# The last pair of heads' column tiles, two at a time: first half of the tokens of both, then the second half of both

## The chip, the cores and the metric

One core of a Trainium2 chip. The time is device microseconds of one execution of the whole program on that core, lower is better. The engines are TensorE (PE: matmuls; PEld: its weight loads), VectorE (DVE), ScalarE (ACT), GpSimd (POOL) and SyncE (SP), which issues the DMAs.

## The reference

A hybrid block on x of 1024 tokens by 1024 channels, all in float32. A normalised input h goes through one wide projection w_in. Its columns feed a gated MLP branch (result ya), an RWKV-7 branch (result yb) and two gates:

```python
p = p + mu * (token_shift(p) - p)          # pb: columns r, k, v, z of the RWKV branch
o = wkv7_scan(r_h, w_h, k_h, v_h, kk, a_h) # 16 heads of 64, one state per head, along 1024 tokens
o = group_norm(o) * gn_g + gn_b + bonus
yb = o * silu(z)
...
merged = sigmoid(ga) * (ya @ w_a) + sigmoid(gb) * (yb @ w_b)
out = x + rms_norm(merged @ w_o, g_post)
```

The token shift reads the token before, so the second half of the tokens needs the last column of the first half.

## The kernel before

Tokens are the free dimension, channels the partitions. Two halves of 512 tokens; a *column tile* is 128 output channels. `gemm` (line 714) makes one column tile of one half: 8 blocks of 128 input channels, three matmuls each of 128x128 against 128x512 (the high parts, high against low, low against high), 24 matmuls into one PSUM bank "ps". The operand of the projections lies in 32 SBUF buffers of one pool ("hm": 8 blocks, high and low part, two halves). A weight column comes through `load_w` (line 701): one DMA to "raw" (one buffer), ACT writes the high part "whi", DVE or POOL the low part "wlo" (two buffers of each).

Stage 1 is the gated MLP. Stage 2 (pool "rw") is the RWKV branch: 8 pairs of heads, p = 0 to 7, each with four column tiles in the order k, r, v, z, and for each pair two *units* (p, h), one per token half, made by `half_unit` (line 426). A column tile is evacuated by `shifted` (line 1027): ACT scales the PSUM bank, DVE adds the bank shifted by one token, and the first half leaves its last column in "edge" for the second half.

A unit (p, h) prepares K, B and the decays; PE makes products of them (W·BK), DVE masks them to Pm and BA; Pm goes through DRAM (bs_d) into X, from which POOL solves a triangular system in 62 instructions on Q and qt; the result goes through DRAM (ts_d) into N; DVE transposes N into Pm, PE makes N·Pm and Pm·N, X·Pm, BA·X, and then a chain of eight small steps (pc<-Z,W) carries the state along the tokens. The normed and gated result oc is stored to yb_d.

Behind the last pair the 32 hm buffers are loaded with ya (ya_d, 32 loads of 256 KB, the first half's 16 first), each when the last matmul that reads the buffer's old content is done. Sixteen gemms with w_a follow (`jobs`); their results are gated on DVE (tile "r") and stored to ma_d. The projections with w_b and w_o are Strassen products (`product`): blocks of yb come back from DRAM, DVE and POOL add and subtract them (the *train* of additions), ACT and DVE split the sums, PE multiplies. w_a's gemms need no yb.

The order of every engine is made when the program is built, by a list scheduler (`Sched.flush`, line 240). Each operation has a priority (chain 0, evacuation and inverse 1, splits and loads 2, dense matmuls 9, last); among the operations that by its model can start soonest on their engine it takes the one of best priority, then the one that comes first in the program. A buffer's next owner waits for its last reader. So dense gemms fill what the units leave free on PE, and the engines run the resulting lists in order. SP's list is one queue: a DMA whose operand is late holds up all DMAs behind it.

Every operation is issued through a helper, so the profile puts all of them on line 134; they are told apart by tile names.

Of the kernel before, what the change touches and what calls it, by code (L numbers as in the profile page):

```python
# [21 lines left out]
KT = D // P  # L22
# [39 lines left out]
class Sched:  # L62
# [45 lines left out]
    @contextlib.contextmanager  # L108
    def at(self, prio):
        old, self.prio = self.prio, prio  # L110
        yield
        self.prio = old
# [544 lines left out]
def body(S, I, out):  # L657
    with contextlib.ExitStack() as stack:
        trunk(S, stack.enter_context, I, out)


def trunk(S, enter, I, out):
# [29 lines left out]
    def col(base, i):  # L692
        return vec[:, base + i:base + i + 1]
# [7 lines left out]
    def load_w(src, page=None, raw_page=None, later=0, hi_eng=None):  # L701
        raw = raw_page(F32) if raw_page else wp.tile([P, 1024], F32, name="raw", bufs=1)
        with at(W_DMA + later):
            dma(raw, src)
        hi, lo = [page(F32R) if page else wp.tile([P, 1024], F32R, name=nm, bufs=2) for nm in ("whi", "wlo")]
        with at(W_SPLIT + later):
            if hi_eng is not None:
                hi_eng.tensor_copy(hi, raw)
            else:
                act(hi, raw, AF.Copy)  # L710
            A.tensor_tensor(lo, raw, hi, op=ALU.subtract)
        return hi, lo
# [13 lines left out]
    def gemm_ct(w, rh, rl, dest=()):  # L726
        for h in range(2):
            ps = gemm(w, rh, rl, h, dest[h:h + 1])
            with at(EVAC):
                yield slice(512 * h, 512 * h + 512), ps  # L730
# [10 lines left out]
    with S.pool("gm") as gp:  # L741
        def page(dtype=F32, shape=(P, T)):
            return gp.tile(list(shape), dtype, name="pg", bufs=17, fifo=False)

        def ring(dtype):
            return gp.tile([P, 1024], dtype, name="ring", bufs=4)
# [4 lines left out]
        for i, n in enumerate((128, 128, 256, 256, 256)):  # L751
# [3 lines left out]
            if n == 128:  # L755
                x = gp.tile([P, KT, n], F32, name="z") if i == 0 else ring(F32).rearrange("p (k n) -> p k n", k=KT)
# [32 lines left out]
        def row(nm, shape=(P, T), dtype=F32, bufs=1):  # L789
            return gp.tile(list(shape), dtype, name=nm, bufs=bufs)  # L790
# [45 lines left out]
        for g in range(KT):  # L836
            for b in range(KT):
                x = vt[g][:, b, :]
# [121 lines left out]
        for d in range(2):  # L960
            w = load_w(I["w_in"][GA + d])
# [33 lines left out]
        for k in range(4):  # L995
            v1, v2 = row("th"), page()
# [25 lines left out]
    with S.pool("rw") as rw:  # L1022
# [1 line left out]
        V.tensor_scalar(hv[:, 0:32], vec[:, V_W0:V_W0 + 32], 0.5, None, op0=ALU.mult)  # L1024
        V.tensor_scalar(hv[:, 32:40], vec[:, V_KA:V_KA + 8], -0.5, 1.0, op0=ALU.mult, op1=ALU.add)

        def shifted(ct, w, tiles):

            for sl, ps in gemm_ct(w, hh, hl, tiles):
                t_ = tiles[0 if sl.start == 0 else 1]  # L1030
                act(t_, ps, AF.Identity, scale=om[:, ct:ct + 1])
                V.scalar_tensor_tensor(t_[:, 1:512], ps[:, 0:511], col(V_MU, ct), t_[:, 1:512],
                                       op0=ALU.mult, op1=ALU.add)
                if sl.start == 0:
                    edge = rw.tile([P, 1], F32, name="edge", bufs=2)
                    V.tensor_scalar(edge, ps[:, 511:512], col(V_MU, ct), None, op0=ALU.mult)
                else:
                    V.tensor_tensor(t_[:, 0:1], t_[:, 0:1], edge, op=ALU.add)

        RW0 = 2 * KT  # L1040
        order = [4 * KT] + [ct for p in range(KT) for ct in (KT + p, p, 2 * KT + p, 3 * KT + p)]

        def dense():

            w = wn
            for i, ct in enumerate(order):
                nw = load_w(I["w_in"][RW0 + order[i + 1]] if i + 1 < len(order) else I["w_a"][0])
                yield ct, w
                w = nw
            yield None, w  # L1050

        tiles = dense()

        xw, xa = rw.tile([P, T], F32R, name="xw"), rw.tile([P, T], F32R, name="xa")
        wa = rw.tile([P, T], F32, name="X", bufs=2, fifo=False)
        shifted(*next(tiles), [wa[:, 0:512], wa[:, 512:1024]])
        act(wa[0:64, :], wa[0:64, :], AF.Tanh)
        act(xw[0:64, :], wa[0:64, :], AF.Copy)
# [17 lines left out]
        for p in range(KT):  # L1076
            def halves(nm, bufs):
                return [rw.tile([P, 512], F32, name=nm, bufs=bufs) for _ in range(2)]

            k2, r2, v2, z2 = halves("k0", 2), halves("r", 3), halves("v", 2), halves("zz", 3)  # L1080
            for x in (k2, r2, v2, z2):
                shifted(*next(tiles), x)
            up = rw.tile([P, 2 * P], F32, name="hk")
            uh, ul = rw.tile([P, 2 * P], F32R, name="uh"), rw.tile([P, 2 * P], F32R, name="ul")
            with at(W_DMA):
                dma(up, I["up"][:, p])
            with at(PREP):
                G.tensor_copy(uh, up)
                A.tensor_tensor(ul, up, uh, op=ALU.subtract)
            for h in range(2):  # L1090
                sl = slice(512 * h, 512 * h + 512)
                Znext = half_unit(S, I, rw, dram, bank, p, h, r2[h], k2[h], v2[h], z2[h], uh, ul, bdr, xw[:, sl], xa[:, sl],
                                  Znext, KI[h], vec, con, hv, eps, yb_d[p][:, sl])
# [11 lines left out]
        _, wn = next(tiles)  # L1105
# [37 lines left out]
        def parts(xs):  # L1143
            return [part(x) for x in xs]
# [7 lines left out]
        def loaded(src):  # L1152
            x = unit()
            with at(W_DMA):
                dma(x, src)
            return x
# [48 lines left out]
        def wo(n):  # L1205

            xs = []
            for k in R4:
                t, hi, lo = pair_tile()
                with at(W_DMA):  # L1210
                    dma(t.bitcast(F32), wo_d[n][k])
                xs.append((hi, lo))
            return xs
# [53 lines left out]
        e2, r2 = parts(f2), wo(1)  # L1267
# [45 lines left out]
        x = {b: [loaded(I["x"][P * b:P * b + P, hs[e]]) for e in range(2)] for b in (0, 1, 2, 3, 4, 5, 6, 7)}  # L1313
# [68 lines left out]
```

## Time and profile before

| | us |
|---|---|
| median of 3 runs | 1429.69 (1426.26 to 1430.96) |
| the profiled execution | 1426.28 |
| its span | 1424.1 |
| PE busy in the span | 1347.4 |
| DVE, ACT, POOL busy | 1118.8, 742.6, 525.8 |

The span runs from the first to the last instruction; 2.2 us of the execution lie around it. The profile gives every instruction's start and duration, what ended the idle time before it, and the clock that was granted to TensorE (1.00 is 2.4 GHz, 0.50 is 1.2 GHz). Busy time on PE includes slow matmuls, so both columns are read together: idle time, and clock.

### The profile page before, as it was taken

The numbers are of one execution on the slowest core, as the hardware profiler recorded it, in microseconds if no ns is written. First come the engines' busy times: TensorE is split into PE (matmuls) and PEld (weight loads), VectorE is DVE, ScalarE is ACT, GpSimd is POOL, SyncE is SP. The second block draws the span as 40 slices with busy tenths as digits, with TensorE's granted clock in tenths as the row PEclk, the third lists the DMA queues.
The fourth block names the chain that finished last, engine by engine and source line by source line (L and its number), as shares of the span: only waits on it lengthen the run. The fifth ranks groups of instructions, "written<-read, shape, count | busy, mean of one in ns | idle before, by whom it ended". The sixth has DMA issues, their size and how long they took to land.

```text
span 1424.1 us, 23358 instructions
## 1 busy us (share of the span) xinstructions
PE 1347.4 (95%) x8390; PEld 1075.0 (75%) x8390; DVE 1118.8 (79%) x2034; ACT 742.6 (52%) x1340; POOL 525.8 (37%) x1135
## 2 busy tenths in 40 slices
PE   5899999999999999999998989999899899979997
PEld 3787888888878777777776767777677677858785
DVE  7977888887865868888788877888788575599957
ACT  6626444444444656667655567666666353433223
POOL 0002000001121176756566663776745553043211
PEclk9899999999999999999999999999999899989999
DMA  7102434447775211222211212211135756254456
GB/s 250 45 1 96 155 134 148 141 140 228 263 249 205 64 56 38 67 71 67 64 46 45 57 53 64 61 54 48 53 99 165 230 177 226 88 202 170 140 215 242
DMA packets 109523, 175.12 MB, mean 123 GB/s; under 512 B 43488, under 2 KB 53856, under 8 KB 109408
## 3 DMA queue, kind: packets, MB, share of 16 engines
q1 hardware_dynamic: 109408, 173.64, 36.8%
q8 instruction: 66, 1.08, 0.3%
q14 instruction: 49, 0.40, 0.1%
HBM read 121.17 MB, written 52.43 MB: 122 GB/s over the span
## 4 chain that ended last, share of the span: by engine, by line
PE 67%; DVE 13%; ACT 9%; DMA 6%; issue 4%; SPq 1%; POOL 1%; DVEq 0%; ACTq 0%; POOLq 0%
PE ps L134 37%; PE pg L134 25%; PE pc L134 5%; DVE hm L134 2%; DVE Pm L134 2%; ACT L134 2%; DVE W L134 1%; DMA hm<-ya_d 1%; DVE pg L134 1%; ACT Z L134 1%; DVE BK L134 1%; DVE wlo L134 1%; SPq L134 1%; ACT BA L134 1%; ACT KI L134 1%
## 5 line engine op out<-in xcount | busy, mean ns | idle before, releaser
L134 PE MATMUL ps<-hm,whi 128*128 128x512 f32 x1616 | 538.7, 405 | 5.3 <-DMA hm<-ya_d 4.7
L134 PEld LDWEIGHTS ps<-hm,whi 128*128 128x128 f32 x1616 | 301.8, 191 | 69.9 <-DMA hm<-ya_d 9.8
L134 PE MATMUL ps<-hm,wlo 128*128 128x512 f32 x808 | 326.8, 405 | 1.1 <-DVE wlo L134 1.1
L134 POOL TENSOR_TENSOR qt<-X,Q 128x60 f32<-128x60 f32 (+24 forms) x496 | 204.5, 412 | 91.3 <-DMA X<-bs_d 39.0
L134 POOL TENSOR_TENSOR Q<-Q,qt 128x60 f32<-128x60 f32 (+24 forms) x496 | 196.1, 395 | 37.9
L134 PEld LDWEIGHTS ps<-hm,wlo 128*128 128x128 f32 x808 | 154.1, 191 | 33.6 <-DVE wlo L134 3.1
L134 PE MATMUL pg<-pg,ring 128*128 128x512 f32 x720 | 168.1, 389 | 0.0
L134 PEld LDWEIGHTS pg<-pg,ring 128*128 128x128 f32 x720 | 135.1, 188 | 28.1
L134 ACT ACT_TABLE_LOAD x75 | 96.2, 1283 | 2.9 <-DVE mv L134 0.9
L134 ACT ACTIVATE whi<-raw 128x1024 fp32r<-128x1024 f32 x64 | 67.4, 1053 | 56.4 <-PE ps L134 30.0
L134 ACT ACTIVATE Z<-pc,gc 64x64 f32<-64x64 f32 x120 | 36.8, 307 | 106.9 <-PE pc L134 104.7
L134 DVE TENSOR_TENSOR wlo<-raw,whi 128x1024 fp32r<-128x1024 f32 x60 | 74.3, 1238 | 10.1 <-ACT whi L134 9.9
L134 POOL TENSOR_TENSOR th<-th 128x512 f32<-128x512 f32 x3 | 4.2, 1406 | 185.2 <-DMA pg<-in_w_o_dram 175.6
L134 ACT ACTIVATE X<-pg 128x512 f32<-128x512 f32 x64 | 36.9, 594 | 43.5 <-PE pg L134 43.0
L134 PE MATMUL ps<-pg,hm 128*128 128x512 f32 x192 | 50.9, 422 | 9.2 <-ACT pg L134 4.4
L134 DVE TENSOR_SCALAR Z<-pc,gc 64x64 f32<-64x64 f32 x120 | 34.8, 290 | 27.1 <-ACT Z L134 19.5
L134 PEld LDWEIGHTS pc<-Z,W 128*128 128x128 f32 x240 | 40.1, 188 | 20.2 <-DVE Z L134 8.3
L134 PEld LDWEIGHTS ps<-pg,hm 128*128 128x128 f32 x192 | 38.3, 202 | 20.2 <-ACT pg L134 5.0
L134 PE MATMUL pc<-Z,W 128*128 128x128 f32 x240 | 50.8, 293 | 1.1 <-ACT Z L134 0.4
L134 POOL TENSOR_TENSOR wlo<-raw,whi 128x1024 fp32r<-128x1024 f32 x4 | 9.9, 2479 | 112.7 <-DVE pg L134 85.0
L134 PE MATMUL pg<-W,BK 64*128 64x128 f32 (+1 forms) x530 | 47.3, 290 | 2.6 <-ACT KI L134 1.6
L134 PEld LDWEIGHTS pg<-W,BK 64*128 64x128 f32 (+1 forms) x530 | 37.7, 187 | 13.9 <-issue 5.4
(793 smaller groups left out, 2738.2 us busy)
## 6 DMA issues: line engine op xcount, KB each, us to landing
raw<-in_w_in_dram SPq DMA_DIRECT2D x65, 512.0 KB, 3.4
X<-bs_d SPq DMA_DIRECT2D x64, 128.0 KB, 2.7
hm<-ya_d SPq DMA_DIRECT2D x32, 256.0 KB, 5.4
wo_d<-sv SPq DMA_DIRECT2D x12, 512.0 KB, 2.7
raw<-in_w_a_dram SPq DMA_DIRECT2D x12, 512.0 KB, 3.3
W<-wo_d SPq DMA_DIRECT2D x10, 512.0 KB, 4.8
sv<-sv_d SPq DMA_DIRECT2D x8, 512.0 KB, 3.3
ya_d<-th SPq DMA_DIRECT2D x8, 512.0 KB, 2.6
```

What stands on the lines that cost most here:

```text
L134: self.calls.append(lambda: getattr(e, op)(*a, **k))
```

## The change

`shifted` becomes a generator, `shifting`, that stops after each half; `shifted` runs it to its end, as before. For p = 0 to 6 nothing changes. For the last pair the tiles are taken two at a time, first k and r, then v and z, and their halves alternate: k0, r0, k1, r1, v0, z0, v1, z1, in place of k0, k1, r0, r1, v0, v1, z0, z1 (the digit is the token half).

```diff
--- before.py
+++ after.py
@@ -1024,7 +1024,7 @@
         V.tensor_scalar(hv[:, 0:32], vec[:, V_W0:V_W0 + 32], 0.5, None, op0=ALU.mult)
         V.tensor_scalar(hv[:, 32:40], vec[:, V_KA:V_KA + 8], -0.5, 1.0, op0=ALU.mult, op1=ALU.add)
 
-        def shifted(ct, w, tiles):
+        def shifting(ct, w, tiles):
 
             for sl, ps in gemm_ct(w, hh, hl, tiles):
                 t_ = tiles[0 if sl.start == 0 else 1]
@@ -1036,6 +1036,11 @@
                     V.tensor_scalar(edge, ps[:, 511:512], col(V_MU, ct), None, op0=ALU.mult)
                 else:
                     V.tensor_tensor(t_[:, 0:1], t_[:, 0:1], edge, op=ALU.add)
+                yield
+
+        def shifted(ct, w, tiles):
+            for _ in shifting(ct, w, tiles):
+                pass
 
         RW0 = 2 * KT
         order = [4 * KT] + [ct for p in range(KT) for ct in (KT + p, p, 2 * KT + p, 3 * KT + p)]
@@ -1078,8 +1083,15 @@
                 return [rw.tile([P, 512], F32, name=nm, bufs=bufs) for _ in range(2)]
 
             k2, r2, v2, z2 = halves("k0", 2), halves("r", 3), halves("v", 2), halves("zz", 3)
-            for x in (k2, r2, v2, z2):
-                shifted(*next(tiles), x)
+            if p < KT - 1:
+                for x in (k2, r2, v2, z2):
+                    shifted(*next(tiles), x)
+            else:
+                for two in ((k2, r2), (v2, z2)):
+                    steps = [shifting(*next(tiles), x) for x in two]
+                    for _ in range(2):
+                        for step in steps:
+                            next(step)
             up = rw.tile([P, 2 * P], F32, name="hk")
             uh, ul = rw.tile([P, 2 * P], F32R, name="uh"), rw.tile([P, 2 * P], F32R, name="ul")
             with at(W_DMA):
```

The scheduler then makes other lists. Up to about 1030 us they are the same on every engine; the places below follow.

PE, from the end of the last pair to the first gemm of w_a. ps is the bank of a gemm, hm its operand (hm_1224 to 1231 and the like: first half of the last pair's operand; from hm_1248 on: ya), whi and wlo the weight column. Before, the end of z0 (ps_810) and the start of the first w_a gemm (ps_817):

```order
L134 MATMUL ps_810<-hm_1227,wlo_1150 128x512
L134 MATMUL ps_810<-hm_1229,whi_1149 128x512
L134 MATMUL ps_810<-hm_1231,whi_1149 128x512
L134 MATMUL ps_810<-hm_1229,wlo_1150 128x512
L134 MATMUL ps_817<-hm_1248,whi_1152 128x512
L134 MATMUL ps_817<-hm_1249,whi_1152 128x512
L134 MATMUL ps_817<-hm_1248,wlo_1153 128x512
```

Now the end of z0 (ps_799), behind which v1 (ps_805) begins:

```order
L134 MATMUL ps_799<-hm_1227,wlo_1150 128x512
L134 MATMUL ps_799<-hm_1229,whi_1149 128x512
L134 MATMUL ps_799<-hm_1231,whi_1149 128x512
L134 MATMUL ps_799<-hm_1229,wlo_1150 128x512
L134 MATMUL ps_805<-hm_1232,whi_1146 128x512
L134 MATMUL pg_807<-W_5307,BK_5315 128x128
```

And now, some forty rows further, the end of v1 and the start of the first w_a gemm:

```order
L134 MATMUL ps_805<-hm_1243,wlo_1147 128x512
L134 MATMUL ps_805<-hm_1245,whi_1146 128x512
L134 MATMUL ps_805<-hm_1247,whi_1146 128x512
L134 MATMUL ps_805<-hm_1245,wlo_1147 128x512
L134 MATMUL ps_817<-hm_1248,whi_1152 128x512
L134 MATMUL ps_817<-hm_1249,whi_1152 128x512
L134 MATMUL pg_814<-sl_5333,bdr_4808 128x512
```

So v1 has moved in between z0 and the w_a gemm.

SP's queue at ya's loads. Before: the last ones of the first half's loads go ahead of this, and ts_d_167 (the solved Q of unit (6,1)) two rows above; X_5343 is X of unit (7,0), N_5348 is N of (6,1):

```order
L134 DMA hm_1264<-ya_d_0_0_75 128x512
L134 DMA hm_1265<-ya_d_1_0_76 128x512
L134 DMA X_5343<-bs_d_166 32x1024 x4
L134 DMA hm_1266<-ya_d_0_0_77 128x512
L134 DMA hm_1267<-ya_d_1_0_78 128x512
L134 DMA hm_1268<-ya_d_0_0_79 128x512
L134 DMA v_5345<-in_w_b_dram 128x512
L134 DMA hm_1269<-ya_d_1_0_80 128x512
L134 DMA hm_1270<-ya_d_0_0_81 128x512
L134 DMA hm_1271<-ya_d_1_0_82 128x512
L134 DMA hm_1272<-ya_d_0_0_83 128x512
L134 DMA N_5348<-ts_d_167 32x8x32 x4
```

Now, from the last load of the first half (hm_1263) on; X_5334 and N_5339 are the same two, ma_d_0_169 stores the result of the first w_a gemm:

```order
L134 DMA hm_1263<-ya_d_1_0_90 128x512
L134 DMA r_5329<-ga_d_0_70 128x512
L134 DMA bs_d_166<-Pm_5320 32x8x32 x4
L134 DMA X_5334<-bs_d_166 32x1024 x4
L134 DMA raw_1154<-in_w_a_dram 128x1024
L134 DMA ts_d_167<-Q_5268 128x256
L134 DMA N_5339<-ts_d_167 32x8x32 x4
L134 DMA Q_5340<-in_q_dram 128x256
L134 DMA yb_d_0_168<-oc_5325 128x512
L134 DMA ma_d_0_169<-r_5303 128x512
L134 DMA hm_1264<-ya_d_0_0_75 128x512
L134 DMA hm_1265<-ya_d_1_0_76 128x512
```

X and N have moved ahead of all loads of the second half, and these behind the store.

SP's queue at the last unit. Before, ts_d_178 is the solved Q of (7,1) and N_5402 its N; the hm<-yb_d rows are loads for the Strassen products:

```order
L134 DMA ts_d_178<-Q_5349 128x256
L134 DMA ma_d_0_179<-r_5388 128x512
L134 DMA hm_1280<-yb_d_0_163 128x512
L134 DMA hm_1281<-yb_d_0_168 128x512
L134 DMA hm_1282<-yb_d_0_177 128x512
L134 DMA hm_1283<-yb_d_0_138 128x512
L134 DMA hm_1284<-yb_d_0_143 128x512
L134 DMA hm_1285<-yb_d_0_148 128x512
L134 DMA hm_1286<-yb_d_0_153 128x512
L134 DMA hm_1287<-yb_d_0_157 128x512
L134 DMA hm_1288<-yb_d_0_163 128x512
L134 DMA N_5402<-ts_d_178 32x8x32 x4
```

Now (ts_d_176, N_5397):

```order
L134 DMA ts_d_176<-Q_5340 128x256
L134 DMA ma_d_0_177<-r_5385 128x512
L134 DMA N_5397<-ts_d_176 32x8x32 x4
L134 DMA raw_1175<-in_w_a_dram 128x1024
L134 DMA r_5398<-ga_d_0_105 128x512
L134 DMA bon_5399<-in_w_b_dram 128x512
L134 DMA yb_d_0_178<-oc_5390 128x512
L134 DMA zz_5400<-yb_d_0_157 128x512
L134 DMA hm_1280<-yb_d_0_163 128x512
```

The loads of yb that stood between ts_d and N have moved behind N.

## Rows read from the trace of the kernel before

**Rows 1.** Section 1 of the page: busy us, share of the span and instructions, by engine

```profile
PE 1347.4 (95%) x8390; PEld 1075.0 (75%) x8390; DVE 1118.8 (79%) x2034; ACT 742.6 (52%) x1340; POOL 525.8 (37%) x1135
```

**Rows 2.** Windows: stretch and length; busy (x instructions) by engine; PE clock, DMA share, GB/s

```profile
1095.00:1128.00 33.00, 28.20 (x171) 19.27 (x170) 18.08 (x31) 12.84 (x18) 14.58 (x42) 0.79 0.97 303
1128.00:1202.00 74.00, 73.72 (x547) 59.90 (x547) 48.45 (x91) 34.45 (x62) 35.86 (x86) 1.00 0.57 185
1202.00:1216.00 14.00, 10.85 (x113) 8.06 (x111) 6.55 (x10) 1.20 (x2) 1.73 (x1) 0.76 0.36 125
...
1266.00:1283.00 17.00, 8.28 (x23) 5.43 (x22) 15.96 (x21) 4.12 (x9) 8.49 (x6) 0.70 0.51 168
```

**Rows 3.** Tile view of ya_d: its loads; who waited for it (us, times)

```profile
L134 SPq DMA_DIRECT2D hm<-ya_d x32: 319/360/881, 1083.3 to 1117.0; - x32
...
  PE ps L134: 4.7, 7
```

**Rows 4.** Timeline of PE: start, us, operation, [idle before, releaser]; earlier unit, ya's wait

```profile
1057.20 1.14 PE L134 MATMUL pg<-N,Pm 32*64 32x32 f32 x32
...
1091.37 0.39 PE L134 MATMUL ps<-hm,wlo 128*128 128x512 f32 x1
1091.60 0.61 PE L134 MATMUL ps<-hm,whi 128*128 128x512 f32 x2
...
1110.52 0.50 PE L134 MATMUL ps<-hm,whi 128*128 128x512 f32 x1 [1.91 <-DMA hm<-ya_d]
...
1111.78 0.63 PE L134 MATMUL ps<-hm,wlo 128*128 128x512 f32 x1
1112.21 0.63 PE L134 MATMUL ps<-hm,whi 128*128 128x512 f32 x1
...
1117.34 0.80 PE L134 MATMUL ps<-hm,whi 128*128 128x512 f32 x1 [1.16 <-DMA hm<-ya_d]
...
1118.49 1.92 PE L134 MATMUL pg<-N,Pm 32*64 32x32 f32 x32
```

**Rows 5.** Timeline of PE: second W·BK group of (7,1), its N·Pm, first wait for the train

```profile
1144.77 1.16 PE L134 MATMUL pg<-W,BK 64*128 64x128 f32 x16
...
1205.33 0.27 PE L134 MATMUL pg<-N,Pm 32*64 32x32 f32 x2 [2.55 <-DVE Pm L134]
...
1272.34 0.79 PE L134 MATMUL pg<-W,W 128*128 128x512 f32 x1 [4.55 <-DVE hm L134]
```

**Rows 6.** Timeline of DVE: last yb tile, start of the train, one add beside POOL

```profile
1241.43 0.69 DVE L134 TENSOR_TENSOR oc<-oc,zz 128x512 f32<-128x512 f32 x1
...
1248.76 0.69 DVE L134 TENSOR_TENSOR hm<-hm,hm 128x512 f32<-128x512 f32 x1 [4.04 <-DMA hm<-yb_d]
...
1263.14 1.78 DVE L134 TENSOR_TENSOR v<-v,oc 128x512 f32<-128x512 f32 x1
```

**Rows 7.** Timeline of ACT: split of the first w_a column, high part

```profile
1082.58 1.06 ACT L134 ACTIVATE whi<-raw 128x1024 fp32r<-128x1024 f32 x1 [0.16 <-PE ps L134]
```

**Rows 8.** Timeline of DVE: split of the first w_a column, low part

```profile
1083.83 1.22 DVE L134 TENSOR_TENSOR wlo<-raw,whi 128x1024 fp32r<-128x1024 f32 x1
```

**Rows 9.** Timeline of POOL: end of (6,1)'s solve, start of (7,0)'s, (7,1)'s first and last

```profile
1094.47 0.22 POOL L134 TENSOR_TENSOR Q<-Q,qt 128x8 f32<-128x8 f32 x1
1110.20 0.25 POOL L134 TENSOR_TENSOR qt<-X,Q 128x31 f32<-128x31 f32 x1 [15.51 <-DMA hm<-ya_d]
...
1156.39 0.70 POOL L134 TENSOR_TENSOR qt<-X,Q 128x31 f32<-128x31 f32 x1
...
1186.54 0.54 POOL L134 TENSOR_TENSOR Q<-Q,qt 128x8 f32<-128x8 f32 x1
```

**Rows 10.** Timeline of SP's queue: loads of X, of N, nine of yb, N again

```profile
1101.86 2.22 SPq L134 DMA_DIRECT2D X<-bs_d  x4
...
1110.51 2.56 SPq L134 DMA_DIRECT2D N<-ts_d  x4
...
1189.87 6.35 SPq L134 DMA_DIRECT2D hm<-yb_d  x9
1196.27 2.62 SPq L134 DMA_DIRECT2D N<-ts_d  x4
```

## The prediction, made before the changed kernel ran

> **What bounds the kernel now.** The page's busy shares come first: TensorE's matmuls (PE) fill 95% of the span, no other engine above 79% [rows 1]. So the kernel is a stream of matmuls with a few holes, and a change of order can gain no more than the holes downstream of it. The change touches nothing before the last pair's gemms (about 1030 us), so I read the rest by stretches [rows 2]. From 1128 to 1202 us PE is busy 73.7 of 74 us at full clock. The time is lost in three places.
>
> Hole A, 1095 to 1128 us: PE is busy 28.2 of 33 us and its mean clock is 0.79, while the DMA engines are 97% busy [rows 2]. The first w_a gemm waits piecewise for its operand, ya, which takes over the buffers that held the last pair's operand: 4.7 us on PE in 7 waits [rows 3], the longest 1.91 us [rows 4]. Shortly after that wait the records show half clock (1.2 GHz) until 1127: starts of 512-column matmuls stand 0.43 us apart instead of 0.23, N·Pm takes 1.92 us where it took 1.14 earlier [rows 4]. Nineteen such matmuls at 0.2 us more are 3.7, N·Pm 0.8, Pm·N 0.4: about 4.8. Hole A is 9.5 us.
>
> Hole B, 1202 to 1216 us: PE is busy 10.85 of 14 us at a mean clock of 0.76 [rows 2]. PE waits 2.55 us for DVE's Pm [rows 5], the transposed inverse N of the last unit, (7,1), and runs at half clock after it. 3.15 us of idleness and about 2.7 of slow matmuls (ten 512-column ones and the first two products, as above): 5.9.
>
> Hole C, 1266 to 1283 us: PE is busy 8.28 of 17 us, DVE 15.96 [rows 2]. PE waits, 4.55 us at first, for a train of DVE additions [rows 5] that starts only once the last unit's output yb has come back from DRAM, 4.04 us after DVE was last busy, and then runs without a gap [rows 6]. 8.7 us idle and some 2.2 at half clock (a mean of 0.70 over 17 us is 10 us of half clock, in which PE worked less than half of the time): 10.9.
>
> **The change part by part.** No instruction is added or removed: eight gemms with their evacuations change places. k0 was first anyway. The work is the same 24 matmuls each, so the edit itself costs nothing on PE, and its generators issue nothing.
>
> *z0 earlier.* Before, z0's last matmul stands directly ahead of the first matmul of the w_a gemm. Now 49 rows stand between (v1's gemm with some recurrence matmuls), 11.3 us by their durations. z0 is the last reader of the first half's 16 buffers, so their 16 loads can start during z0. At the 303 GB/s of rows 2 these 4.2 MB take 13.8 us, and a w_a gemm reads its last buffer 5.5 us after its first (24 matmuls of 0.23). First loads about 1 us after z0's start, z0 7 us long: the last lands near 10 us after z0's end, against a need at 11.3 (first) to 17 us (last). Hole A's waits and their half clock go: −9.5.
>
> *Given back there.* (1) The weight buffers of the first w_a column are v's, and v1 now ends right ahead of it. Its two splits then stand on the path: 1.06 us on ACT [rows 7] and 1.22 on DVE [rows 8], less the 0.7 us of matmuls that need only the first: about 2 us with the hand-overs (before, z0's gemm hid them). (2) N·Pm of (6,1) stands 6 us earlier on PE while its POOL solve does not move: 0 to 2, I take 1. (3) The second half's 16 loads now stand on SP's queue behind the last Q of (6,1), its N, and the store ma_d of the first w_a gemm. They start about 1.5 us after that gemm ends, the second w_a gemm 31 rows (some 8 us) after it; a pair of loads takes 1.75 us at the rate of rows 2 and some 2 more for the first, a pair's share of that gemm and what stands in it 1.6 us (13 over 8), so the last pair is needed about 2 us after it lands. 0 to 4, I take 1. (4) No half clock to follow; if the 2 us hole brings one, up to 3 more. Sum +4 (0 to +9), so A nets −5.5.
>
> *The last solve.* POOL ended (6,1) at 1094.7 and then stood 15.51 us before (7,0), because X came late [rows 9]: SP issued X's loads at 1101.86 among the ya loads, and N's at 1110.51 [rows 10]. Now X and N of these units stand ahead of the second half's loads, so (7,0) can start near 1095 to 1098. But (7,1) gains less: its solve started at 1156.39 [rows 9], after the second W·BK group at 1144.77 [rows 5] had been evacuated and sent through DRAM. That group stands 3.2 us earlier in PE's stream, plus the holes' 6: near 1135. The solve can start near 1147, ends near 1178 (1156.39 to 1187.1 was 30.7 us, rows 9), and its N no longer stands behind nine yb loads that held SP for 6.35 us [rows 10]: ready for PE near 1187 instead of 1205. PE however comes to N·Pm of (7,1) earlier as well: 48 matmuls, 11 us, plus the holes: near 1185. So hole B shrinks to about 4 with its half clock (0 to 11): −2.
>
> *The train.* The last unit's chain stands 11 us earlier in a stream that has no other gap. DVE's train, 33 us long from 1248.76 [rows 6], can start near 1227 to 1232, while the dense matmuls before the products that need it end at about the same count as before (1244 less what A and B gave). PE's need for the first sums comes at 1272 less some 7; the train's matching sum at 1272 less 17 to 21. Hole C shrinks to about 2 (0 to 9): −9. What bounds it then is DVE: adds with both inputs in SBUF took up to 1.78 us beside POOL's adds, against 0.69 alone [rows 6]; four of them did, which is 4.4 us of the train. The Trainium skill ("SBUF — State Buffer", section "Who interferes with whom") says that a DVE instruction with two SBUF inputs contends with a GpSimd instruction that reads SBUF; the trace agrees, 1.78 against 0.69 us. It speaks against the gain, since POOL's share of the train moves along with it: by the rule each further add that meets POOL's costs 1.1 us, and four more would leave C at 6 instead of 2.
>
> Sum: −5.5 −2 −9 = −16.5. I keep 1.5 back for the tail, where the two engines are evenly loaded. So −15 on the profiled execution's own 1426.3 us (span 1424.1 and 2.2 around it), 1411.3. The median of the runs is 3.4 above that execution, so 1414.7, say 1414.5.
>
> **The rivals.** (a) *Hole A only moves.* Hole A nets −5.5 and nothing follows: the train starts early but PE arrives as early, so that B and C keep their size. For it: PE's stream is reordered everywhere by the planner, and each hole is a race of two moves of about 10 us. Against it: N's delay behind yb loads and X's behind ya loads were queueing on SP, and both are gone from the order. 1424 or so: between same and faster.
>
> (b) *Same.* DVE is busy 15.96 of 17 us in hole C [rows 2]; if the products are bound by its adds and the slowed ones grow in number, C keeps 8 us, and the split wait, N of (6,1) and a half clock eat A's gain. 1427 to 1430.
>
> (c) *Slower: the second half's loads.* They stand on SP behind the last Q of (6,1), N and ma_d, in one queue. If POOL ends (6,1)'s solve later than before relative to PE, or raw's load ahead of them (which waits for the split of the first w_a column) is late, each us of it delays all 16 loads by one, and PE stops in the second w_a gemm. The margin worked out above is about 2 us at the last pair, 3 to 4 at the first. From about 15 us of lateness on, the loss (12 us idle, a third more for half clock) passes the whole gain worked out above; at 19 to 23 us it is +5 to +10, 1434 to 1440. Against it: POOL ended (6,1) at 1094.7 [rows 9], and the first w_a gemm now ends near 1098, so ma_d, not Q, comes last.
>
> (d) *The clock gives it back.* A wait of 1.91 us was followed by 16 us of half clock [rows 4]. The split wait in front of the first w_a gemm is of that size, and so is what I leave of B and C. If each brings a stretch like that, 4 to 5 us each: 1424 to 1428. The Trainium skill ("TensorE: Matmul & The Clock Gate", section "HAM oscillation — how this bites in real kernels") says that gaps in PE's work bring the throttle back and every stretch after them starts cold; the half clock behind the waits of rows 4 agrees, though there were several waits close together there, and one wait alone is not shown by it.
>
> That the order does not change is excluded by the instruction order itself: the second w_a gemm, all recurrence groups of the last pair and the loads stand elsewhere.
>
> **How the numbers follow.** The forecast (at least two of three holes shrink, 1405 to 1421) 0.58; (a) 0.13; (d) 0.10; (b) 0.10; (c) 0.09. A measurement of this kernel can tell about 0.3% (4.3 us) from no change. Faster by more than that: the forecast, two thirds of (a) and half of (d), 0.72; same: the rest of (a) and (d) and most of (b), 0.17; slower: (c) and a little of (b), 0.11. The range: all holes at their best end (−9.5 −5.9 −10.9, about −26) is 1403.5; I take 1405 at the low end, with little left out there, and 1428 at the high one, which takes in (a) and (d) and leaves out (c) and most of (b).
>
> **What would show it.** Right: no PE wait on ya's loads above 0.5 us and full clock through the first w_a gemm except for a wait of about 2 us on its split; POOL's gap before (7,0) under 4 us; N of (7,1) directly behind its store, PE's wait there under 3 us; DVE's train starting ahead of 1235 and PE's waits on it under 3 us. Wrong: a PE wait on ya in the second w_a gemm (then c); a train that starts early but PE's wait unchanged (then b, and DVE beside POOL is the bound); new half-clock stretches behind waits of 2 us (then d).

## The result, and the profile after

| | before | after |
|---|---|---|
| median | 1429.61 us, 4 runs (1426.26 to 1430.96) | 1408.38 us, 4 runs (1406.05 to 1413.82) |
| ratio | | 0.986 (0.9826 to 0.9895) |
| the profiled execution | 1426.28 | 1409.79 |
| its span | 1424.1 | 1408.0 |

Faster by 1.4%. The median was forecast at 1414.5; on the profiled execution −15 was forecast and −16.5 came. Run once more (first experiment below) the ratio was 0.9865.

The first section of the page of the changed kernel (busy us, share of the span, instructions), to be read against [rows 1]:

```profile
PE 1339.3 (95%) x8390; PEld 1071.6 (76%) x8390; DVE 1114.3 (79%) x2026; ACT 745.6 (53%) x1342; POOL 535.6 (38%) x1143
```

PE runs the same 8390 matmuls and is busy 8.1 us less: matmuls that ran at half clock before run at full clock now. DVE counts eight instructions fewer and POOL eight more: besides the order, the scheduler has changed who does what, and net eight operations went from DVE to POOL. The windows of the changed kernel (stretch, length, busy time and instructions of PE, PEld, DVE, ACT, POOL, then PE's clock, DMA share, GB/s), against [rows 2]:

```profile
1095.00:1128.00 33.00, 31.15 (x249) 24.29 (x247) 26.23 (x51) 18.85 (x33) 25.30 (x62) 0.95 0.70 238
1128.00:1202.00 74.00, 73.06 (x601) 57.74 (x600) 47.05 (x89) 32.24 (x55) 29.37 (x66) 1.00 0.60 194
1202.00:1216.00 14.00, 14.00 (x91) 11.05 (x91) 8.95 (x14) 8.50 (x15) 3.73 (x2) 1.00 0.40 140
...
1244.00:1266.00 22.00, 17.36 (x64) 13.61 (x63) 21.20 (x24) 10.10 (x19) 11.77 (x7) 0.84 0.35 115
```

Hole A is mostly closed (28.2 busy at 0.79 before, 31.15 at 0.95 now) and hole B is gone. Hole C stands earlier, at 1255 to 1260, and is smaller. The waits of PE behind these figures, from its timeline (start, us, operation, idle time before it and its releaser), against [rows 4, 5]:

```profile
1092.77 0.73 PE L134 MATMUL ps<-hm,whi 128*128 128x512 f32 x2 [0.92 <-ACT whi L134]
...
1094.03 0.50 PE L134 MATMUL ps<-hm,wlo 128*128 128x512 f32 x1 [0.29 <-DVE wlo L134]
...
1114.94 1.74 PE L134 MATMUL pg<-BA,X 64*128 64x128 f32 x16 [1.82 <-ACT X L134]
1116.61 0.79 PE L134 MATMUL ps<-hm,whi 128*128 128x512 f32 x1
...
1185.43 1.12 PE L134 MATMUL pg<-N,Pm 32*64 32x32 f32 x32
...
1197.63 0.49 PE L134 MATMUL pc<-Z,W 128*128 128x128 f32 x2 [0.70 <-DVE W L134]
...
1259.83 1.22 PE L134 MATMUL ps<-wlo,raw 128*128 128x512 f32 x2 [4.64 <-DVE wlo L134]
```

No row waits for ya. In its place stand the split of the first w_a column (0.92 and 0.29) and, in the second w_a gemm, a wait for X of unit (6,1) (1.82) with some 3.4 us of half clock behind it (a mean clock of 0.95 over 33 us). N·Pm of the last unit starts at 1185.43 with nothing in brackets. One wait for the train of additions is left, 4.64, where there were three.

SP's queue says why, against [rows 10]:

```profile
1071.48 1.28 SPq L134 DMA_DIRECT2D hm<-ya_d  x3
...
1073.32 9.07 SPq L134 DMA_DIRECT2D hm<-ya_d  x13
...
1092.16 1.70 SPq L134 DMA_DIRECT2D X<-bs_d  x4
...
1098.06 2.82 SPq L134 DMA_DIRECT2D N<-ts_d  x4
...
1102.59 4.06 SPq L134 DMA_DIRECT2D hm<-ya_d  x8
...
1177.08 0.32 SPq L134 DMA_DIRECT2D ts_d<-Q  x1
...
1178.80 2.56 SPq L134 DMA_DIRECT2D N<-ts_d  x4
```

The first sixteen loads of ya are issued by 1082.4; X leaves at 1092.16 where it left at 1101.86, N of (6,1) at 1098.06 for 1110.51, N of (7,1) at 1178.80 for 1196.27. POOL follows, against [rows 9]: the first instruction of (7,0)'s solve, the first of (7,1)'s, the last of (7,1)'s:

```profile
1096.51 0.25 POOL L134 TENSOR_TENSOR qt<-X,Q 128x31 f32<-128x31 f32 x1 [1.85 <-DMA X<-bs_d]
...
1149.08 0.25 POOL L134 TENSOR_TENSOR qt<-X,Q 128x31 f32<-128x31 f32 x1 [1.85 <-DMA X<-bs_d]
...
1176.83 0.22 POOL L134 TENSOR_TENSOR Q<-Q,qt 128x8 f32<-128x8 f32 x1
```

**Where the 16.1 us of span came from.** From 1030 us on PE has 9.1 us less idle time and 6.9 us less busy time. By hole, with the loss to half clock estimated from the lengths of the slow matmuls, as in the prediction: A 2.3 idle and 3.8 of half clock, 6.1; B 2.5 and 2.7, 5.2; C 4.1 idle (8.7 to 4.64), less 0.4 more at half clock, 3.7. That makes 15.0; 1.1 us is spread over the rest.

### The profile page after: what moved, and what is told of

Read it like the earlier page. It is cut to its first block, busy times and chain, and to the rows that moved or that the text cites. A ratio compares the mean times of both kernels' runs of the same rounds, so it can differ in the third digit from the quotient of the medians.

```text
span 1408.0 us, 23363 instructions
## 1 busy us (share of the span) xinstructions
PE 1339.3 (95%) x8390; PEld 1071.6 (76%) x8390; DVE 1114.3 (79%) x2026; ACT 745.6 (53%) x1342; POOL 535.6 (38%) x1143
## 4 chain that ended last, share of the span: by engine, by line
PE 63%; DVE 14%; ACT 9%; DMA 6%; issue 4%; SPq 1%; POOL 1%; DVEq 0%; ACTq 0%; POOLq 0%
PE ps L134 36%; PE pg L134 23%; PE pc L134 5%; DVE hm L134 3%; DMA wo_d<-sv 2%; DVE Pm L134 1%; DVE W L134 1%; ACT L134 1%; SPq L134 1%; ACT Z L134 1%; DVE pg L134 1%; DVE wlo L134 1%; ACT KI L134 1%; ACT BA L134 1%; DVE BK L134 1%
## 5 line engine op out<-in xcount | busy, mean ns | idle before, releaser
L134 POOL TENSOR_TENSOR Q<-Q,qt 128x60 f32<-128x60 f32 (+24 forms) x496 | 199.2, 402 | 37.8
```

Source lines behind the costliest of these rows:

```text
L134: self.calls.append(lambda: getattr(e, op)(*a, **k))
```

## The experiments

Ratios are to runs of the kernel before on the same chip. Where only one thing was to move, the lists that the scheduler had made were edited by hand, `move(list, engine, operations, anchor)`, and merged again. Those diffs show that call alone; numbers are operations in program order.

**The change again.** The kernel as changed, a second time.

> The changed kernel once more, beside the experiments of this call, so that they are compared on one chip. Every theory: 16 to 21 us below before.

0.9865 (0.9849 to 0.988), −19.3 us. Its profile has the same waits (0.92 and 0.30 on the split, 1.49 for X, 4.93 for the train) and the tail is as long: from an N·Pm near 1014 us, up to which both programs are the same, to the end it is 392.9 us in the first profile, 393.2 here and 409.6 before. "The tail" below is this stretch.

**One pair of tiles alone.** Only v and z alternate:

```diff
-                for two in ((k2, r2), (v2, z2)):
-                    steps = [shifting(*next(tiles), x) for x in two]
-                    for _ in range(2):
-                        for step in steps:
-                            next(step)
+                for x in (k2, r2):
+                    shifted(*next(tiles), x)
+                steps = [shifting(*next(tiles), x) for x in (v2, z2)]
+                for _ in range(2):
+                    for step in steps:
+                        next(step)
```

> Only v and z of the last pair alternate (k0, k1, r0, r1, v0, z0, v1, z1). Theory (three holes): z0 still ends one gemm ahead of the first w_a gemm, and N*Pm of the last unit stands 49 matmuls earlier than before, so holes A, B and C shrink as in the changed kernel: 16 to 21 us below the kernel before, within 4 us of the changed kernel. Rival (the alternation of k and r carries part of it, because it brings the last pair's preparation forward): less than 12 us below before.

0.9885 (0.9864 to 0.9907), −16.4 us, tail 389.7. The same edit for k and r, with v and z as before:

> Only k and r of the last pair alternate; z0 again ends directly ahead of the first w_a gemm, while N*Pm of the last unit stands about 42 matmuls (9.6 us) earlier than before. Theory (three holes): the wait for ya with its half clock stays, 7 to 10 us, hole B and C shrink: 7 to 12 us below before. Rival (all of the gain comes from the last unit's chain standing earlier, the wait for ya costs nothing at the end): 16 to 21 us below before, as the changed kernel.

0.9922 (0.9905 to 0.9938), −11.1 us, tail 398.4. PE still waits for ya there, four times and 2.3 us in all, 3.50 at the state chain (pc<-Z,W), and 5.3 for the train. So v and z carry the change, as expected. That k and r add to it is not shown: the interval of v and z alone overlaps the changed kernel's, and their tail (389.7) is some 3 us shorter than its two. The two gains do not add up (27.5 against some 20), since both draw on holes A and C.

**N out of the yb loads, in the kernel before.** This does by hand what I held to be the cause of hole B: N's loads go directly behind the store of Q, and DVE's transposes ahead of its additions.

```diff
+def edit(plan, q):
+    move(q, "SP", [9801, 9802, 9803, 9804], 9800)
+    move(q, "DVE", [9805, 9806, 9807, 9808], 10598, behind=False)
```

> The kernel before with two places of its lists exchanged by hand: SP issues the last unit's four loads of N directly behind their store, ahead of the nine loads of yb, and DVE's four transposes of N stand ahead of the additions that wait for these loads; nothing else moves. Theory: hole B (2.55 us and 0.60 us of waiting and half clock, 5.9 in all) goes, and since the last unit sets when yb and the train of additions come, hole C only moves along: 4 to 6 us below before, PE's wait at N*Pm under 0.5 us. Rival (the train and not PE sets the end, so that hole C grows by what B loses): within 1.5 us of before.

1.0018 (1.0004 to 1.0032): no gain. The timeline of PE has no wait at N·Pm, but one step on:

```profile
1211.77 1.07 PE L134 MATMUL pg<-Pm,N 64*32 64x32 f32 x32 [5.87 <-DVE N L134]
```

And DVE's timeline, where N<-pg is the masked copy that PE waits for:

```profile
1204.85 0.69 DVE L134 TENSOR_TENSOR g__0_5356<-hm,g__0_5356 128x512 f32<-128x512 f32 x1 [3.93 <-DMA hm<-yb_d]
...
1210.63 0.69 DVE L134 TENSOR_TENSOR hm<-hm,hm 128x512 f32<-128x512 f32 x1
1211.23 0.48 DVE L134 TENSOR_SCALAR N<-pg,con 128x256 f32<-128x256 f32 x1
```

The copy stands in DVE's list behind seven additions that wait for the yb loads, and these now come after N. Nor is N itself much earlier: SP issues it at 1194.83 (before: 1196.27), 6.0 us after the store of Q, because that store is slow to land. The view of DMA issues around it (KB each, us from issue to landing):

```profile
ts_d<-Q SPq DMA_DIRECT2D x1, 128.0 KB, 5.9
```

and the same view of the changed kernel:

```profile
ts_d<-Q SPq DMA_DIRECT2D x1, 128.0 KB, 1.7
```

In the first, SP has just issued a w_a column of 512 KB, the yb store and three more loads; in the changed kernel those go out behind N. My theory of hole B, N behind nine loads and nothing else, was wrong.

**The seven additions out of the way as well:**

```diff
+def edit(plan, q):
+    move(q, "SP", [9801, 9802, 9803, 9804], 9800)
+    move(q, "DVE", [9805, 9806, 9807, 9808], 10325, behind=False)
+    move(q, "DVE", [10598, 10600, 10602, 10604, 10630, 10632, 10634], 9843)
```

> As the experiment that put the last unit's N first in the kernel before, but DVE's seven additions that wait for yb stand behind all of DVE's steps between N and X*Pm (transposes, masked copy, copies), not only behind the transposes. Theory: the last unit's steps were caught in DVE's list behind additions that wait for loads; with all of them ahead, hole B (5.9 us) goes and the rest moves along: 4 to 6.5 us below before. Rival (hole C absorbs what B loses): within 1.5 us of before.

0.9998 (0.9983 to 1.0013): again none. PE comes without a wait through all four products of the last unit and stops at its state chain:

```profile
1222.52 0.80 PE L134 MATMUL pc<-Z,W 128*128 128x128 f32 x2 [4.49 <-DVE W L134]
```

DVE's steps on W stand behind the split of a w_a column, whose load SP issues at 1212.98, behind ten yb loads and three stores; the last of them ahead of PE's start ends at 1222.47:

```profile
1219.04 1.23 DVE L134 TENSOR_TENSOR wlo<-raw,whi 128x1024 fp32r<-128x1024 f32 x1 [4.35 <-ACT whi L134]
1220.18 0.42 DVE L134 TENSOR_TENSOR W<-pg,KI 128x256 f32<-128x256 f32 x1
...
1222.05 0.42 DVE L134 TENSOR_TENSOR W<-pg,KI 128x256 f32<-128x256 f32 x1
```

Hole B thus has several late items one behind the other: the store's landing, the yb loads with the additions that wait for them, a w_a column with its split, each with a step of the unit behind it in DVE's list. Taking one away moves the wait to the next. In the changed kernel all of them have changed places.

**N late again, in the changed kernel.** N of (7,1) is issued eight DMAs later, behind, among others, three loads of yb and two stores:

```diff
+def edit(plan, q):
+    move(q, "SP", [9801, 9802, 9803, 9804], 10272)
```

> The changed kernel with one place exchanged by hand: SP issues the last unit's loads of N seven DMAs later, behind three loads of yb and the store ma_d that waits for a w_a gemm; nothing else moves. SP came to that place at 1186 us instead of 1179. Theory: PE waits 5 to 7 us at N*Pm of the last unit, with 2 to 3 us of half clock behind it, and nothing later gives it back: 7 to 10 us above the changed kernel. Rival (hole C is a wait for DVE's additions, which does not depend on the last unit, and absorbs it): 0 to 3 us above the changed kernel.

0.9936 (0.9917 to 0.9955), so by the ratios about 10 us of the changed kernel's gain are gone; the tail, 399.6, is 6.5 us longer. SP issues N at 1180.64, and PE's timeline has the wait back, with half clock behind it (1.91 us for an N·Pm of 30):

```profile
1186.16 0.39 PE L134 MATMUL pg<-N,Pm 32*64 32x32 f32 x2 [4.82 <-DVE Pm L134]
1187.03 1.91 PE L134 MATMUL pg<-N,Pm 32*64 32x32 f32 x30 [0.48 <-DVE Pm L134]
```

An early N is needed for hole B to go, and does not do it alone.

**z0 ahead of v1, in the kernel before.** The two gemms change places by hand, their evacuations too, and the first half's loads are put together on SP. The rest of the order stays.

```diff
+def edit(plan, q):
+    v1, z0 = list(range(9261, 9285)), list(range(9291, 9315))
+    at = sorted(q["PE"].index(i) for i in v1 + z0)
+    both = [i for i in q["PE"] if i in z0] + [i for i in q["PE"] if i in v1]
+    for n, i in zip(at, both):
+        q["PE"][n] = i
...
+    loads = list(range(9977, 9993))
+    move(q, "SP", loads[1:], 9977)
```

> The kernel before with the gemms of v1 and z0 exchanged by hand on PE (with their evacuations on ACT and DVE, and the split of the first w_a column behind v1's), and the first half's 16 loads of ya issued together; the recurrence, X and N stand where they stood. This is hole A's part of the change alone. Theory: PE's waits on the first half of ya go, about 2 us of waiting on the split come, and as X's and N's loads still stand among the second half's loads, PE waits 2 to 4 us for these: 3 to 6 us below before, holes B and C as before. Rival (A's loads only move the wait to the second half of ya): within 1.5 us of before.

0.9982 (0.9966 to 0.9999), −2.6 us, between the two. The waits of the first w_a gemm are gone but for its split (1.96 and 0.56). In exchange PE waits four times in the second, 4.3 us in all; the longest:

```profile
1117.30 0.50 PE L134 MATMUL ps<-hm,whi 128*128 128x512 f32 x1 [1.69 <-DMA hm<-ya_d]
```

Its timeline of SP shows X and N in the middle of the second half's sixteen loads:

```profile
1101.87 0.98 SPq L134 DMA_DIRECT2D hm<-ya_d  x2
1103.03 2.01 SPq L134 DMA_DIRECT2D X<-bs_d  x4
...
1109.93 2.93 SPq L134 DMA_DIRECT2D N<-ts_d  x4
...
1113.68 3.66 SPq L134 DMA_DIRECT2D hm<-ya_d  x7
```

In the changed kernel both are ahead of them all (1092.16 and 1098.06), and the products of (6,1) fill PE while the loads land (N·Pm at 1104.11, X·Pm at 1108.51). Here the second half is late, and B and C have the sizes of before.

**z0 and v1 exchanged back, in the changed kernel:**

```diff
+def edit(plan, q):
+    z0, v1 = list(range(9264, 9288)), list(range(9291, 9315))
+    at = sorted(q["PE"].index(i) for i in v1 + z0)
+    both = [i for i in q["PE"] if i in v1] + [i for i in q["PE"] if i in z0]
+    for n, i in zip(at, both):
+        q["PE"][n] = i
...
```

> The changed kernel with the gemms of z0 and v1 exchanged back by hand on PE (with their evacuations), so that z0 ends directly ahead of the first w_a gemm; SP's list stays, but for one load of w_b that moves ahead of ya's loads. Theory (the first half of ya has to be freed a gemm ahead, and X, N and the second half queue behind it on SP): PE waits 4 to 6 us for ya with half clock behind it, and X and N come later too: 6 to 14 us above the changed kernel. Rival (as the exchange alone brought the kernel before only 1 to 3 us, z0's place is worth no more here): 0 to 3 us above the changed kernel.

0.9937 (0.9915 to 0.9958): about 10 us lost. The loads of ya start 12 us later and hold SP, whose timeline is

```profile
1083.54 11.65 SPq L134 DMA_DIRECT2D hm<-ya_d  x16
...
1102.78 1.75 SPq L134 DMA_DIRECT2D X<-bs_d  x4
...
1108.74 2.82 SPq L134 DMA_DIRECT2D N<-ts_d  x4
```

PE waits not for ya but for N of (6,1), behind it in the queue:

```profile
1113.78 0.39 PE L134 MATMUL pg<-N,Pm 32*64 32x32 f32 x2 [7.06 <-DVE Pm L134]
```

Its stretch from 1095 to 1128 is back at 24.40 us busy and a clock of 0.79. So z0's early place is worth about 10 us in the whole order and 2.6 without the rest of it.

**The last yb tile early, in the kernel before.** The train's first addition takes the tile of the seventh pair instead of that of the last, so that it waits for no unit; this leaves the last pair's data out of one sum. The tile's load and the six w_b loads behind it move forward on SP.

```diff
-            return [loaded(yb_d[4 * j + k][:, hs[h]]) for k in R4]
+            early = S.plan is not None and j == h == 1
+            return [loaded(yb_d[6 if early and k == 3 else 4 * j + k][:, hs[h]]) for k in R4]
...
+    move(q, "SP", [10529, 10530, 10531, 10532, 10533, 10534, 10535], 10447)
```

> The kernel before with the last unit's tile of yb replaced by the sixth pair's (the products of that tile are left out in this sense), so that its load needs no store, and with this load and six loads of w_b moved ahead in SP's queue, to 1228 us; nothing else moves. Theory: hole C was set by the arrival of the last unit's yb 5 us behind the end of the dense gemms; the train then starts at their end, near 1245 instead of 1248.8, PE's waits at hole C fall from 8.7 to 4 or 5 us and the half clock shrinks: 4 to 6 us below before, what the earlier chain brings the changed kernel at hole C. Rival (hole C is the train's own order and length): within 1.5 us of before.

0.996 (0.9945 to 0.9976), −5.7 us. DVE's train starts without the gap of [rows 6], and PE's three waits for it are 1.93, 1.18 and 3.12, 6.2 in all for 8.7. Hole C is in part the round trip of the last yb tile; the waits shrink by 2.5 us only. In this profile hole B was smaller as well (0.60), so not all of its 7.9 us of shorter tail (401.7 for 409.6) is hole C's; it is also the fastest of the nine runs, 5.9 us below their median.

**What is left of hole C.** The timeline of DVE in the changed kernel, from the train's first addition to the wait of 4.64:

```profile
1228.63 0.69 DVE L134 TENSOR_TENSOR hm<-hm,hm 128x512 f32<-128x512 f32 x1 [0.61 <-DMA hm<-yb_d]
...
1243.45 0.68 DVE L134 TENSOR_TENSOR v<-v,hm 128x512 f32<-128x512 f32 x1
...
1244.66 1.79 DVE L134 TENSOR_TENSOR hm<-hm,hm 128x512 f32<-128x512 f32 x1
1246.37 1.78 DVE L134 TENSOR_TENSOR Pm<-Pm,hm 128x512 f32<-128x512 f32 x1
...
1253.18 1.78 DVE L134 TENSOR_TENSOR raw<-hm,raw 128x512 fp32r<-128x512 f32 x1
...
1259.09 0.68 DVE L134 TENSOR_TENSOR wlo<-hm,wlo 128x512 fp32r<-128x512 f32 x1
```

Seven additions take 1.75 to 1.79 us where their neighbours take 0.68; the timeline of POOL has additions in the same stretch:

```profile
1244.33 1.56 POOL L134 TENSOR_TENSOR whi<-r,whi 128x512 fp32r<-128x512 f32 x1 [1.35 <-PE pg L134]
1245.86 1.74 POOL L134 TENSOR_TENSOR xa<-hm,xa 128x512 fp32r<-128x512 f32 x1
```

Two edits of the changed kernel ask whether DVE's order or POOL's company sets the wait. First the order: seven subtractions that later products need go behind the last split of the stalled one.

```diff
+def edit(plan, q):
+    move(q, "DVE", [10783, 10784, 10785, 10786, 10787, 10788, 10789], 10629)
```

> The changed kernel with seven DVE additions of the train, whose results are needed only by later products, moved by hand behind the last split that the product at hole C waits for (0.6 us each, 4.2 us in all). Theory: hole C is the length of DVE's train between the end of the dense gemms and that split; PE's wait of 4.6 us falls to 0 to 1 us and the half clock behind it goes: 3 to 6 us below the changed kernel. Rival (the sums are needed soon after, the wait moves to the next products): within 1.5 us of the changed kernel.

0.9848 (0.9824 to 0.9871), 3.1 us below the changed kernel on the same chip (1405.08 for 1408.16), tail 384.5. PE's wait at C is 0.27, and its clock is 1.00 from 1244 to 1283. With four runs each the medians do not part the two kernels clearly (the intervals of their ratios overlap); that the wait is gone, the profile shows. The edit does not part order from company either: five of the seven are among the slow additions, and in their new place they take 0.68 us each, while POOL's addition beside them takes 5.04 where it took 1.30. Then POOL's company: eight of POOL's operations go to DVE, at their places in the order.

```diff
+    to_dve(plan, q, [10617, 10621, 10625, 10627, 10701, 10703, 10711, 10769], pos)
```

> The changed kernel with eight additions of the train given to DVE instead of POOL, at their places in the order (1240 to 1256 us of the changed kernel's trace, where seven of DVE's adds took 1.78 us instead of 0.68). Theory (DVE's adds are slow because POOL's run beside them): DVE gets eight adds of 0.6 us more, 4.8 us, and loses 7 x 1.1 = 7.7 us, so PE's wait at hole C falls from 4.6 to about 2 us: 1 to 4 us below the changed kernel. Rival (the slow adds have another cause, DVE only gets more work): 4 to 6 us above the changed kernel.

1402.67 us against 1428.05, 0.9814 (0.9792 to 0.9835), −26.6 us: about 7 below the changed kernel (0.9865, on another chip), tail 386.4 for 393. DVE has more to do and is done sooner. Its timeline, beginning with the same additions:

```profile
1243.86 0.68 DVE L134 TENSOR_TENSOR hm<-hm,hm 128x512 f32<-128x512 f32 x1
...
1246.87 0.68 DVE L134 TENSOR_TENSOR raw<-hm,raw 128x512 fp32r<-128x512 f32 x1
...
1252.28 0.68 DVE L134 TENSOR_TENSOR wlo<-hm,wlo 128x512 fp32r<-128x512 f32 x1
```

The last row is the same split that came at 1259.09. PE has no idle time there; the window of this kernel (columns as above):

```profile
1244.00:1266.00 22.00, 22.00 (x96) 17.84 (x95) 21.97 (x36) 12.84 (x23) 2.69 (x2) 1.00 0.56 180
```

It has the lowest median of the study, though not clearly: its interval overlaps that of the seven subtractions, whose tail is shorter (384.5). I had expected 1 to 4 us, too little: the whole rest of hole C went, 4.6 of idle time and some 2.5 of half clock. Both edits together:

> The changed kernel with both edits: seven additions that are needed later moved behind, and eight of POOL's additions given to DVE. Theory: the first edit has closed hole C already (PE's wait 0.3 us), so the second gains nothing more: 2 to 6 us below the changed kernel, within 2 us of the first edit alone. Rival (the slowed adds cost something in the later products as well): 2 us or more below the first edit alone.

0.984 (0.9813 to 0.9868), no better than either alone. C's wait is gone, but the subtractions put off are needed later. PE's timeline:

```profile
1269.82 1.22 PE L134 MATMUL pg<-W,BA 128*128 128x512 f32 x2 [2.99 <-DVE W L134]
```

## Why the prediction came out as it did

It was right: faster, inside its range, 6 us below the number. About 1.5 of the 6 are the trace's. The rest is luck, the step from one execution to the median: before, the profiled execution was 3.4 us below the median, and I added that; after, it is 1.4 above.

**Hole A** (−5.5 forecast, −6.1 measured). The steps held: z0's loads went early, no wait on ya is left, the split's wait came as named (1.21 for 2), and the gemm ran at full clock. But the sum hides an error. There was no wait for the second half of ya and none at N·Pm of (6,1) (I had 1 us for each). What came back was a step not in the list, BA·X of (6,1) waiting 1.82 us for ACT's copy of X, with some 3.4 us of half clock behind it. The copy stands in ACT's list behind the split of a w_b column (tile v), whose load SP issues in the middle of the second half's ya loads and which lands 7 us later. From the timelines of SP and ACT in the changed kernel:

```profile
1106.74 0.39 SPq L134 DMA_DIRECT2D v<-in_w_b_dram  x1
...
1113.77 0.63 ACT L134 ACTIVATE xw<-v 128x512 fp32r<-128x512 f32 x1 [2.14 <-DMA v<-in_w_b_dram]
1114.31 0.58 ACT L134 ACTIVATE X<-pg 128x512 f32<-128x512 f32 x1
```

The forecast followed the chain of (6,1) to N·Pm only, not to its last product, and asked of the second half's loads only when they land, not what stands among them in the queue.

**The last solve** held to 2 us at each point: second W·BK at 1135.18 (1135 forecast), the solve from 1149 to 1177 (1147 to 1178), PE at N·Pm at 1185.43 (1185).

**Hole B** (−2 forecast, −5.2 measured). The mis-sized term is N's readiness: 1187 was forecast. POOL's solve ended 1 us ahead of its forecast (1177.05 for 1178), DVE's transposes took 1.81 us from 1183.65, and N·Pm started at 1185.43 straight on. N moved by 19.9 us (from 1205.33) and PE by 17.4 (from 1202.78, where its wait began), and the 1.6 us that N was better than forecast decided over the whole hole. That N came so early has a cause I had not seen: its store landed in 1.7 us, where the store before took 5.7, and N followed it by 1.72 us. In the profiles of the kernel before and its four edits the last store of Q goes out right behind the w_a column, the yb store and the three loads, and lands in 5.6 to 6.0 us; in the other nine it lands in 1.7. The cause that I gave, N behind nine yb loads, is a part: without them the kernel before gained nothing (1.0018, and 0.9998 with the additions moved too), and with N late again the changed kernel had the wait back.

**Hole C** (−9 forecast, −3.7 measured). The train started at 1228.6 and ran from 1233, as forecast. The failed step is PE's need. I took the first wait of the hole and let the train gain 17 to 21 us against PE's 7. The first two waits (4.55 and 0.88) went. But they had been holding PE back from the third, which the timeline of PE before has as

```profile
1278.10 1.22 PE L134 MATMUL ps<-wlo,raw 128*128 128x512 f32 x2 [3.29 <-DVE wlo L134]
```

PE reached that product, ps<-wlo,raw, at 1274.8 before (1278.10 less 3.29) and at 1255.2 now, 19.6 us earlier. Its operand came 18.3 us earlier, so the wait grew to 4.64, above the 3 us that the prediction allowed for being right. A hole of three waits has to be followed to its last one.

The bound beyond it was named rightly, DVE beside POOL: seven slow additions for four, 7.7 us of train, and without POOL's eight operations the hole was gone. The Trainium skill ("SBUF — State Buffer", section "Who interferes with whom") gives this contention as a rule; 0.68 against 1.78 us in the two kernels agrees.

**The rivals.** (a), the hole only moves, is what the exchange of two gemms alone does (−2.6 us, the wait in the second half), not the whole change. (b) was half right: the slowed additions grew in number, and C kept 4.6 us of wait. (c) did not come: no row of the second w_a gemm waits for ya. (d) came in part: some 3.4 us of half clock behind the wait of 1.82 and some 7 behind that of 4.64 (0.84 over 22 us), none behind the split's. Its measure was also too long: at hole A before, a mean of 0.79 over 33 us [rows 2] is some 14 us of half clock, not 16.

The three misses (more gained by 0.6 on A and 3.2 on B, less by 5.3 on C) nearly cancel, which is luck, so the good total says less than the holes.

## What to carry to other kernels

Where an engine runs a fixed list, a wait that is taken away alone shows up at the next late item; ask of every hole what the second and third items are waiting for before crediting its removal. Look for the queue behind several holes at once: moving one last reader 12 us forward let sixteen loads leave the DMA queue early, and in the new order the loads of a solve and of an inverse went ahead of the next sixteen; the same move without that order brought 2.6 us. Giving operations to a second engine can cost more than it saves where the two slow each other: eight operations moved back to the busier engine gained about 7 us, though none on top of an order that had already closed the hole.

## What the runs showed of the hardware

A single wait of PE was not always followed by half clock. Of the waits for X in one place, 1.82 us (the changed kernel) and 1.61 (both edits of C) were followed by some 3.4 us of it (a mean clock of 0.72 from 1114 to 1120 us in both); 1.63 (eight operations on DVE) and 1.49 (the change again) by none, with a granted clock of 1.00. With eight operations on DVE a wait of 2.43 us at the state chain was followed by none either; with v and z alone, 0.60 at N·Pm of (7,1) was followed by some 3.4 us (a mean of 0.86 from 1180 to 1192). The kernel before had seven waits of 4.7 us in all at hole A [rows 3], and some 14 us at half clock. What decides it is open.

The part of the program that no edit touches varied more than several of the effects: the N·Pm near 1014 us started between 1013.07 and 1017.98 in the fourteen profiles. For the changed kernel, profiled twice, the tails from there on agree better (0.3 us apart) than the spans (1.7). But a tail is that of one execution: those of v and z alone and of the seven subtractions are shorter than their medians would have it.
